# A decoder block on one core: high weight parts by a casting transfer of GpSimd's queue

## The chip, the cores and the metric

The kernel runs on one core of a Trainium2 chip, in one launch. The metric is device time in microseconds, the median of the runs. A profile of one execution stands beside it: engines are TensorE (PE, with its weight loads as PEld), VectorE (DVE), ScalarE (ACT), GpSimd (POOL) and SyncE (SP). SP and POOL issue transfers: SP on a hardware queue (q1 in the profile), POOL on a software queue (q0).

## The reference

One layer over 512 positions of width 1024, everything in float32:

```
h = rmsnorm(x)
[q | k | v | u_pool | u_gate] = h @ w_in            # 1024 x (1024+1024+1024+512+2048)
A = diff_attention(q, k, v)                         # 8 heads, two softmaxes each, causal
P = multiscale_pool(u_pool)                         # 4 groups, windows 2, 4, 8, 16
x = x + (sigmoid(g_A) * A + sigmoid(g_P) * P) @ w_out
x = x + relu(rmsnorm(x) @ w_up)^2 @ w_down          # 1024 -> 4096 -> 1024
return rmsnorm(x)
```

## The kernel before

Every product is made from parts: a float32 operand is split into a high part in the format float32r, which PE multiplies in one pass, and a low part, the rest, in the same format. A product is then three matmuls, high by high, high by low and low by high. Weights come in blocks of 128 x 1024 (512 KB), and each block has a high tile `wh_...` and a low tile `wl_...`. Both have four buffers that are used in turn, so a block's tiles can be filled while the three blocks before it are multiplied.

There are two ways to split a block, both in `get_w`. `load_w` issues a raw copy on SP's queue into a raw tile (`wr_...`, two buffers of tag `wr`; every third load, by the counter `nraw`, takes the one buffer of tag `wr3` while the first stage's memory is open) and allocates the high and low tiles.

- With an engine given (V for DVE), `split_w` casts the raw tile to the high one on ACT (L112) and subtracts on DVE (L113). This is the way of the query and key blocks (`proj` called by `qk`), of the four blocks of the second half of the output columns and of blocks 1 and 3 of the first half.
- With "dma" given, ACT casts the raw tile to the high one (L120), ACT writes its negative into the low tile (L121), and POOL issues a transfer that adds the weights from HBM once more onto the low tile (L122). This is the way of the 4 blocks of the pool branch (`pool`, tiles `wh_u`), the 16 gate blocks (`gate`, tiles `wh_ga` and `wh_gp`) and blocks 0 and 2 of the first half of the output columns (tiles `wh_o`): 22 blocks.

A projection block (`proj`, `mm3`) runs 16 matmuls of 512 columns with the high tile (L131, L132) and then 8 with the low one (L135). An output block (`mm_rows`, L581 to L583) takes high, low, high in turn, so it needs both tiles at once.

The stages in order of time: the norm and the value projection (to about 58 us); queries, keys, pool branch, gates and attention, head by head, with the pool and gate blocks as fillers between the heads by the list `LAG` (to 300 us); the output product in two halves of columns and the second norm (to about 350 us); then the up and down projections in four rounds, with their sums and differences of blocks also made by transfers of POOL's queue. Per head, POOL also computes two elementwise products for the norm of the head's output (L426, L427), whose result PE reads at L430, the window sums of the pool branch (L452) and a gate product (L481).

The order of instructions on each engine is not written by hand. A planner at build time simulates the engines, starts instructions as they become ready and allocates buffers; a few `after` edges fix an order where the text wants one. At run time each engine works strictly in that order and waits on semaphores, POOL's transfers included.

Of the kernel before, what the change touches and what calls it, by code (L numbers as in the profile page):

```python
# [12 lines left out]
F32R = mybir.dt.float32r  # L13
# [5 lines left out]
P = 128  # L19
# [32 lines left out]
def block_kernel(ctx, tc, xT, x_tok, gains, pos, consts, w_in, w_v, w_pool, w_out, w_up, w_dn, out):  # L52
    nc = tc.nc
    V, A, G, T = nc.vector, nc.scalar, nc.gpsimd, nc.tensor
# [12 lines left out]
    wp = ctx.enter_context(tc.tile_pool(name="wp", bufs=1))  # L67
# [22 lines left out]
    def f(ap):  # L90
        return ap.bitcast(F32)
# [4 lines left out]
    def load_w(src, name, nsplit=1, parts=None):  # L96

        nraw[0] += 1
        third = nraw[0] % 3 == 0 and ctx1_open
        raw = (tp if third else wp).tile([P, 1024], F32, tag="wr3" if third else "wr", name=f"wr_{name}", bufs=1 if third else 2)  # L100
        if nsplit == 1:
            nc.sync.dma_start(out=raw, in_=src)
        else:
            w = 1024 // nsplit
            for i in range(nsplit)[parts or slice(None)]:
                nc.sync.dma_start(out=raw[:, i * w : (i + 1) * w], in_=src[:, i * w : (i + 1) * w])
        hi = wp.tile([P, 1024], F32R, tag="wh", name=f"wh_{name}", bufs=4)
        lo = wp.tile([P, 1024], F32R, tag="wl", name=f"wl_{name}", bufs=4)
        return raw, hi, lo

    def split_w(raw, hi, lo, sl=slice(0, 1024), eng=None):
        ins = A.copy(out=hi[:, sl], in_=raw[:, sl])  # L112
        (eng or G).tensor_tensor(out=lo[:, sl], in0=raw[:, sl], in1=f(hi)[:, sl], op=ALU.subtract)  # L113
        return ins

    def get_w(src, name, eng=None):
        raw, hi, lo = load_w(src, name)
        if eng == "dma":

            A.copy(out=hi, in_=raw)  # L120
            A.mul(out=lo, in_=f(hi), mul=-1.0)  # L121
            G.dma_start(out=lo, in_=src, accum_op=ALU.add)  # L122
        else:
            split_w(raw, hi, lo, eng=eng)
        return hi, lo

# [15 lines left out]
    for i in range(2):  # L142
# [22 lines left out]
        out=mask[:, 384:512], in_=mask[:, 384:512], pattern=[[-1, P]],  # L165
# [51 lines left out]
    for n in range(2):  # L217
        accs = [bank((0, 1, 2, 3, 4, 5, 6, 0)[4 * n + t], f"v{n}_{t}") for t in range(NT)]
        for kk in range(4):
            if n == 0:  # L220
                xprep(2 * kk)
            if n == 0 and kk == 0:
                raw, hi, lo = wv0
                nc.sync.dma_start(out=raw[:, 512:], in_=w_v[0, 0, :, 512:])
            else:
                raw, hi, lo = load_w(w_v[n, kk], f"v{n}_{kk}", 2 if n == 0 else 1)
# [33 lines left out]
        for t in range(NT):  # L260
# [4 lines left out]
                out=vd[2], in0=av, scalar=rcol[:, t, 0:1], in1=vd[1],  # L265
# [26 lines left out]
        out=r_, in0=posf.rearrange("p (t o) -> p t o", o=1).to_broadcast(sh),  # L292
# [63 lines left out]
    def proj(m, name, eng=None):  # L356
        hi, lo = get_w(w_in[m], name, eng)
        a_ = acc(name)
        mm3(a_, hi, lo, xh, xl)
        return a_  # L360
# [245 lines left out]
    for kk in range(4):  # L606
        w = get_w(w_out[0, kk], f"o0_{kk}", V if kk % 2 else "dma")
        for k in (2 * kk, 2 * kk + 1):
            for t in range(NT):
                mm_rows(po[t], t, k, w, k == 0, k == NK - 1)  # L610
    for t in range(NT):
        nc.sync.dma_start(out=x1[:, t, :], in_=x_tok[t])
    for t in range(NT):
        x1_add(t, 0, po[t])
        row_early(t, 0)
    g2b, _ = gain(R[4].rearrange("p b c -> p (b c)"), 0)
    ws = [get_w(w_out[1, kk], f"o1_{kk}", V) for kk in range(4)]
    for t in range(NT):
        a_ = bank(4 + t, f"po1_{t}")
# [19 lines left out]
        for b in range(t // 2, 2):  # L639
            hi, lo = (gab[b][:, t // 2, i, :, sl] for i in range(2))  # L640
# [352 lines left out]
```

## Time and profile before

| | |
|---|---|
| median of 3 runs | 676.17 us (675.97 to 676.85) |
| span of the profiled execution | 675.2 us |
| PE busy | 665.3 us, 99% |
| DVE, ACT, POOL busy | 529.1, 462.5, 123.0 us |
| moved by q0 (POOL) and q1 (SP) | 38.80 MB and 69.38 MB |

The profiled execution has only its span of 675.2 us, from the first instruction to the last; the median is about 1 us above it. In the views below, a window row gives the stretch, its length, the busy time of PE, PEld, DVE, ACT and POOL with counts, then the granted PE clock, the busy share of the DMA engines and GB/s. A row of waits gives who waited for whom: us in total, times, longest. A group row gives line, engine, operation, tiles (written <- read), count, then busy us and mean ns of one. A row of one tile or line gives durations as minimum/median/maximum in ns. Rows in order of time begin with start and duration in us.

### The profile page before, as it was taken

How to read it: one execution, taken by the hardware profiler on the slowest of the kernel's cores; microseconds unless marked ns; L12 is line 12 of the kernel's file. 1: busy time of each engine (PE TensorE's matmuls, PEld its weight loads, DVE VectorE, ACT ScalarE, POOL GpSimd, SP SyncE). 2: the span in 40 equal slices, each digit the busy share in tenths (PEclk: the TensorE clock that was granted, in tenths of full speed). 3: DMA queues.
4: the chain of work that ended last, by engine and by line, in shares of the span. 5: the costliest groups of instructions: out<-in, count | busy, mean ns of one | idle time of the engine just before them, and what ended most of it. 6: DMA issues, size and time to landing. Idle time of an engine off the chain costs nothing.

```text
span 675.2 us, 9995 instructions
## 1 busy us (share of the span) xinstructions
PE 665.3 (99%) x3686; PEld 579.9 (86%) x3686; DVE 529.1 (78%) x879; ACT 462.5 (68%) x741; POOL 123.0 (18%) x137
## 2 busy tenths in 40 slices
PE   9999999999999999999999999999999999999995
PEld 7788888888888888888889988899889998899884
DVE  6955877799979986975478989667994599747995
ACT  8465587978887698883477975367753696356874
POOL 6201110132133212520201020202103021210120
PEclk9999999999999999999999999999999999999999
DMA  8526574435254364574964678676969579493863
GB/s 272 189 71 182 126 152 125 102 94 126 87 139 105 101 171 94 126 193 177 309 194 79 196 172 241 153 179 155 234 190 197 200 156 260 125 213 131 213 125 124
DMA packets 32880, 109.34 MB, mean 162 GB/s; under 512 B 4032, under 2 KB 4928, under 8 KB 32832
## 3 DMA queue, kind: packets, MB, share of 16 engines
q0 software_dynamic: 10656, 38.80, 32.4%
q1 hardware_dynamic: 21744, 69.38, 29.0%
q8 instruction: 29, 0.48, 0.3%
q10 hardware_dynamic: 432, 0.52, 0.2%
q14 instruction: 19, 0.16, 0.1%
HBM read 106.59 MB, written 2.10 MB: 161 GB/s over the span
## 4 chain that ended last, share of the span: by engine, by line
PE 86%; DMA 5%; issue 5%; DVE 1%; ACT 1%; SPq 0%; DVEq 0%; POOLq 0%
PE dm L838 7%; PE dm L840 7%; PE dm L841 7%; PE um L759 7%; PE um L764 7%; PE um L761 7%; DMA wga_uNone<-w_up 5%; PE o L417 2%; PE ga L132 2%; PE ga L131 2%; PE gp L135 2%; PE k L132 2%; PE gp L132 2%; PE gp L131 2%; PE k L131 2%
## 5 line engine op out<-in xcount | busy, mean ns | idle before, releaser
L840 PE MATMUL dm<-wh_dt,z 128*128 128x512 f32 (+1 forms) x128 | 49.5, 387 | 0.0
L841 PE MATMUL dm<-wl_dt,z 128*128 128x512 f32 (+1 forms) x128 | 49.4, 386 | 0.0
L838 PE MATMUL dm<-wh_dt,z 128*128 128x512 f32 (+1 forms) x128 | 49.0, 387 | 0.0
L759 PE MATMUL um<-gss,wh_ut 128*128 128x256 f32 x192 | 48.1, 284 | 0.1
L761 PE MATMUL um<-gss,wh_ut 128*128 128x256 f32 x192 | 48.1, 283 | 0.0
L400 ACT ACTIVATE p<-p,st 128x128 f32<-128x128 f32 (+3 forms) x64 | 35.8, 560 | 14.1 <-DVE st L396 13.8
L112 ACT CAST wh_ut<-wga_uNone 128x1024 fp32r<-128x1024 f32 x24 | 24.9, 1053 | 28.8 <-PE dm L840 19.2
L856 DVE TENSOR_TENSOR x<-x,dm 128x512 f32<-128x512 f32 x48 | 32.8, 687 | 14.1 <-PE dm L841 14.0
L670 POOL DMA_DIRECT2D wga_dNone<-w_dn x16 | 14.2, 887 | 151.8 <-DVE wl_dt L113 151.8
L113 DVE TENSOR_TENSOR wl_ut<-wga_uNone,wh_ut 128x1024 fp32r<-128x1024 f32 x24 | 29.0, 1224 | 12.5 <-ACT wh_ut L112 12.5
L112 ACT CAST wh_ub<-wr_u 128x1024 fp32r<-128x1024 f32 x24 | 25.1, 1051 | 19.0 <-PE um L761 10.1
L670 POOL DMA_DIRECT2D wga_uNone<-w_up x18 | 15.6, 867 | 120.9 <-DVE wl_ut L113 86.9
L840 PE MATMUL dm<-wh_db,z 128*128 128x512 f32 x96 | 37.2, 389 | 0.0
L841 PE MATMUL dm<-wl_db,z 128*128 128x512 f32 x96 | 37.2, 389 | 0.0
L759 PEld LDWEIGHTS um<-gss,wh_ut 128*128 128x128 f32 x192 | 36.8, 192 | 0.3 <-ACT rawz L776 0.3
L761 PEld LDWEIGHTS um<-gss,wh_ut 128*128 128x128 f32 x192 | 36.9, 192 | 0.0
L838 PE MATMUL dm<-wh_db,z 128*128 128x512 f32 x96 | 35.8, 390 | 0.0
L113 DVE TENSOR_TENSOR wl_ub<-wr_u,wh_ub 128x1024 fp32r<-128x1024 f32 x24 | 29.2, 1222 | 7.9 <-ACT wh_ub L112 7.9
L112 ACT CAST wh_dt<-wga_dNone 128x1024 fp32r<-128x1024 f32 x24 | 24.8, 1050 | 14.6 <-issue 4.1
L735 DVE TENSOR_TENSOR z<-rawz,z 128x1024 fp32r<-128x1024 f32 x28 | 33.7, 1225 | 0.9 <-ACT z L732 0.9
L396 DVE CUSTOM_DVE_ANT_0 p<-s,mask 128x128 f32<-128x128 f32 (+3 forms) x64 | 30.3, 485 | 3.4 <-PE s L395 3.3
L732 ACT CAST z<-rawz 128x1024 fp32r<-128x1024 f32 x28 | 28.7, 1048 | 6.0 <-DVE rawz L741 4.9
(324 smaller groups left out, 2222.9 us busy)
## 6 DMA issues: line engine op xcount, KB each, us to landing
wr_u<-w_up SPq DMA_DIRECT2D x24, 512.0 KB, 5.3
wr_d<-w_dn SPq DMA_DIRECT2D x24, 512.0 KB, 4.2
wga_uNone<-w_up POOLq DMA_DIRECT2D x18, 512.0 KB, 6.7
wga_dNone<-w_dn POOLq DMA_DIRECT2D x16, 512.0 KB, 5.8
wr_k<-w_in SPq DMA_DIRECT2D x8, 512.0 KB, 3.3
wr_ga<-w_in SPq DMA_DIRECT2D x8, 512.0 KB, 3.3
wr_gp<-w_in SPq DMA_DIRECT2D x8, 512.0 KB, 4.2
wl_ga<-w_in POOLq DMA_DIRECT2D x8, 512.0 KB, 5.5
```

The source lines that it names most:

```text
L112: ins = A.copy(out=hi[:, sl], in_=raw[:, sl])
L113: (eng or G).tensor_tensor(out=lo[:, sl], in0=raw[:, sl], in1=f(hi)[:, sl], op=ALU.subtract)
L131: T.matmul(acc, lhsT=hi[:, c], rhs=rh[:, k, :], start=k == 0, stop=False)
L132: T.matmul(acc, lhsT=hi[:, c], rhs=rl[k], start=False, stop=False)
L400: A.activation(out=pr[:, c, :N], in_=pr[:, c, :N], func=AF.Exp, scale=-1.0, bias=st[:, c : c + 1], accum_out=st[:, 2 + c : 3 + c])
L735: V.tensor_tensor(out=z[:, 1], in0=r, in1=f(z[:, 0]), op=ALU.subtract)
L759: m = T.matmul(a_, lhsT=hi[:, c], rhs=rh[:, k, :], start=p + k == 0 and onto is None, stop=False, skip_group_check=True)
L761: T.matmul(a_, lhsT=hi[:, c], rhs=rl[:, k, :], start=False, stop=False, skip_group_check=True)
L764: m = T.matmul(a_, lhsT=lo[:, c], rhs=rh[:, k, :], start=False, stop=k == 3, skip_group_check=True)
L838: m = T.matmul(a_, lhsT=zh, rhs=hi[:, sl], start=p == 0 and start, stop=False, skip_group_check=True)
L840: T.matmul(a_, lhsT=zl, rhs=hi[:, sl], start=False, stop=False, skip_group_check=True)
L841: end = T.matmul(a_, lhsT=zh, rhs=lo[:, sl], start=False, stop=p == 3, skip_group_check=True)
```

## The change

In `get_w`, the "dma" way no longer calls `load_w`. It allocates the high and low tiles itself, lets a transfer of POOL's queue bring the weights from HBM into the high tile, where the change of type from float32 to float32r makes it a casting transfer, and goes on as before: ACT writes the negative, POOL's second transfer adds the weights. The raw tile, its copy on SP's queue, the count in `nraw` and ACT's cast fall away for the 22 blocks. The other way is the same.

```diff
     def get_w(src, name, eng=None):
-        raw, hi, lo = load_w(src, name)
         if eng == "dma":
-
-            A.copy(out=hi, in_=raw)
+            hi = wp.tile([P, 1024], F32R, tag="wh", name=f"wh_{name}", bufs=4)
+            lo = wp.tile([P, 1024], F32R, tag="wl", name=f"wl_{name}", bufs=4)
+            G.dma_start(out=hi, in_=src)
             A.mul(out=lo, in_=f(hi), mul=-1.0)
             G.dma_start(out=lo, in_=src, accum_op=ALU.add)
         else:
+            raw, hi, lo = load_w(src, name)
             split_w(raw, hi, lo, eng=eng)
         return hi, lo
```

## The prediction

> **What bounds the kernel now.** I read the page's busy line first, then the windows by stage, then who TensorE (PE) waits for.
>
> ```profile
> PE 665.3 (99%) x3686; PEld 579.9 (86%) x3686; DVE 529.1 (78%) x879; ACT 462.5 (68%) x741; POOL 123.0 (18%) x137
> ```
> ```profile
> 0.00:25.00 25.00, 23.37 (x98) 19.38 (x99) 19.31 (x23) 18.21 (x33) 15.37 (x24) 1.00 0.73 243
> ...
> 75.00:300.00 225.00, 224.94 (x1089) 187.97 (x1088) 190.53 (x441) 183.32 (x347) 59.07 (x58) 1.00 0.50 121
> 300.00:350.00 50.00, 50.00 (x233) 41.56 (x232) 29.33 (x48) 25.89 (x47) 4.76 (x5) 1.00 0.74 237
> 350.00:400.00 50.00, 49.01 (x378) 46.92 (x379) 44.18 (x51) 41.05 (x62) 6.97 (x8) 1.00 0.59 146
> ...
> 650.00:675.20 25.20, 18.00 (x91) 15.22 (x89) 17.11 (x41) 12.47 (x35) 0.00 (x0) 0.94 0.40 120
> ```
> ```profile
> PE warm L170 <- POOL onesr L159: 1.1, 1, 1.1
> PE h2T L629 <- ACT h2f L646: 0.6, 1, 0.6
> PE um L759 <- ACT gss L602: 0.3, 1, 0.3
> PE v L237 <- DVE con L282: 0.3, 1, 0.3
> PE v L235 <- ACT wh_v L112: 0.2, 1, 0.2
> ```
>
> The columns of the windows are PE, weight loads, DVE, ACT, POOL, granted clock, DMA share and GB/s. The changed transfers feed blocks that PE multiplies in the stretch 75 to 315 us. There PE is busy 224.94 us of 225 and 50.00 of 50, at clock 1.00. The waits of PE name no weight of the pool branch, of a gate or of the first output columns: 2.5 us in all, none of it in a touched place. What PE loses lies at the two ends (1.6 us in the first 25 us, 7.2 us in the last 25) and one microsecond between 350 and 400, and the diff is in none of the three. So the kernel is a PE stream without holes where it is changed: a saving on ACT, SP or the queues is not time unless it shortens the stream, and an operand that comes late is time at once.
>
> A busy PE is not PE at its peak, so I bound what a hidden wait could still be worth by the mean duration of one multiplication of 512 columns, in the touched stage (gate and key blocks) and in the down projection:
>
> ```profile
> L131 PE MATMUL ga<-xh,wh_ga 128*128 128x512 f32 x64 | 25.3, 395 | 0.0
> L131 PE MATMUL k<-xh,wh_k 128*128 128x512 f32 x64 | 25.1, 392 | 0.0
> ...
> L840 PE MATMUL dm<-wh_dt,z 128*128 128x512 f32 x124 | 48.3, 390 | 0.0
> ```
>
> Gate against down projection, that is 5 ns for one; over the 1089 matmuls of 75 to 300 us it is 5.4 us. It is the most that a better fed PE could win there, and most of it is not waiting: the long ones follow on short transposes and scores of attention, which stay.
>
> **The change part by part.** 22 blocks take the "dma" way: 4 of the pool branch, 16 gates, 2 of the first output columns.
>
> ```profile
> L120 ACT CAST wh_gp<-wr_gp x8: 1036/1046/1055, 78.6 to 275.0; 128x1024 fp32r<-128x1024 f32 x8
> ...
> L121 ACT ACTIVATE wl_gp<-wh_gp x8: 1054/1062/1067, 80.1 to 278.3; 128x1024 fp32r<-128x1024 f32 x8
> ...
> L122 POOL DMA_DIRECT2D wl_gp<-w_in x8: 847/876/889, 82.6 to 279.6; - x8
> ...
> DMA to landing us min/median/max: 5.2/5.4/7.2
> ```
> ```profile
> 60.00:300.00 240.00, 21.95 (x21) 1.00 0.51 124
> ```
> ```profile
> q0 software_dynamic: 3117, 11.39, 28.7%
> q1 hardware_dynamic: 5184, 18.09, 22.3%
> ...
> wr_gp<-w_in SPq DMA_DIRECT2D x8, 512.0 KB, 4.2
> ```
>
> *Cast removed.* 22 casts of ACT by 1.046 us are 23.0 us; the second row, L120's own time from 60 to 300 us, has 21.95 for 21 of them. ACT is busy 183.32 of 225 us, so this lowers it to about 162. On the path that sets the end it is worth 0: PE never waited for such a cast. What ACT and DVE then do sooner (softmax, weight splits) PE takes no sooner, because it is full.
>
> *Raw copy removed.* 22 issues leave SP's queue, and the raw buffers (two of one tag, every third load in another) turn among the q, k and remaining output blocks alone, which come earlier. The count that picks every third load runs over fewer calls, so other loads get the third buffer. Worth 0: nothing on PE waited for a raw copy.
>
> *Casting transfer added.* 22 issues on POOL by 0.876 us are 19.3 us, and POOL is busy 59.07 of 225. How long one takes to land the trace does not show by itself. From below it is the raw copy of the same 512 KB by SP's queue, 4.2 us median (gp); from above the accumulating transfer of POOL's queue, 7.2 us at the most; the median 5.4 I take, because that one has the same queue, the same source and the same float32 to float32r pair, and only reads its destination besides. On the DMA engines the two queue rows of 60 to 300 us give the price: 28.7% of 240 us for 11.39 MB is 3.2 us of all sixteen for one block of 0.524 MB, 22.3% for 18.09 MB is 1.55. The move costs between 0 and 22 x 1.65 = 36 us of engine time, so the DMA share of that stretch goes from 0.51 to 0.66 at the most: room enough, 0 on the path.
>
> *New chain before PE.* Before, a block's cast started as soon as its high buffer was free. Afterwards that moment starts a transfer: issue and landing 5.4, negation on ACT 1.06, accumulating transfer 5.4 = 11.9 us until the low part is there, with the 0.88 us of an issue and a wait of about 1 us behind ACT's work some 13.8 us. The cover is the four buffers in turn. How long it is, two late blocks show (ACT's order of time, then PE's):
>
> ```profile
> 274.98 1.05 ACT L120 CAST wh_gp<-wr_gp 128x1024 fp32r<-128x1024 f32 x1
> ...
> 279.61 1.05 ACT L120 CAST wh_o<-wr_o 128x1024 fp32r<-128x1024 f32 x1
> ```
> ```profile
> 288.42 0.39 PE L131 MATMUL ga<-xh,wh_ga 128*128 128x512 f32 x1
> ...
> 294.48 0.40 PE L131 MATMUL gp<-xh,wh_gp 128*128 128x512 f32 x1
> ...
> 295.31 0.48 PE L430 MATMUL ss<-sql,onesr 128*128 128x512 f32 x1
> ...
> 298.83 1.98 PE L135 MATMUL gp<-xh,wl_gp 128*128 128x512 f32 x8
> 300.65 0.39 PE L581 MATMUL po<-wh_o,vh 128*128 128x512 f32 x1
> 300.87 0.39 PE L582 MATMUL po<-wl_o,vh 128*128 128x512 f32 x1
> ```
>
> The gate's cast starts at 274.98 and PE reads its high part at 294.48, its low part at 298.83: cover 19.5 and 23.9 us. The output block's starts at 279.61, and PE reads the low part at 300.87, right behind the high one: cover 21.3. Less the chain, 10.1 and 7.5 us stay for queueing on POOL. If that cover were gone, each microsecond of lateness would be a microsecond of the span.
>
> *What stands behind the new waits on POOL.* POOL works in order. It now also waits for a high buffer (released by PE), and its wait for the negation includes a landing. Queued behind are the window sums of the pool branch (L452), the gate products (L481), and the two that PE wants soon, L426 and L427, the squares of a head's output:
>
> ```profile
> 275.29 1.48 POOL L452 TENSOR_TENSOR pa<-u 128x512 f32<-128x512 f32 x1 [2.46 <-DVE u L444]
> 276.84 1.10 POOL L452 TENSOR_TENSOR pb<-pa 128x512 f32<-128x512 f32 x1
> 278.03 1.04 POOL L452 TENSOR_TENSOR pa<-pb 128x512 f32<-128x512 f32 x1
> 279.61 0.87 POOL L122 DMA_DIRECT2D wl_gp<-w_in  x1 [0.54 <-ACT wl_gp L121]
> 280.22 1.58 POOL L452 TENSOR_TENSOR pb<-pa 128x512 f32<-128x512 f32 x1
> 283.77 1.67 POOL L481 TENSOR_TENSOR o<-o,g 128x512 f32<-128x512 f32 x1 [1.96 <-DVE o L435]
> 285.38 0.88 POOL L122 DMA_DIRECT2D wl_o<-w_out  x1
> 291.58 1.12 POOL L426 TENSOR_TENSOR sqo<-o 128x512 f32<-128x512 f32 x1 [5.32 <-ACT o L421]
> 292.78 2.16 POOL L427 TENSOR_TENSOR sql<-sqo,sqh 128x512 fp32r<-128x512 f32 x1
> 296.08 0.88 POOL L122 DMA_DIRECT2D wl_o<-w_out  x1 [1.15 <-ACT wl_o L121]
> ```
>
> L427 ends at 294.94 and PE reads its result at 295.31 (the ss row above): 0.4 us to spare. But POOL had idled 5.32 us in front of L426. The order of every engine is laid out at build time by a planner that starts what is ready, so as a rule a high transfer goes out while POOL would idle, ahead of an accumulation that is not due. I take 0 here.
>
> The sum: 0 from ACT, 0 from SP, 0 from the DMA engines, 0 from POOL's order. The profiled span is 675.2 us and the median of the runs 676.17, about 1 us more around it. Forecast 676.2 us. A difference of 0.2%, 1.35 us, is about what can be told from none here: "same" is 674.8 to 677.5.
>
> **The rivals.**
>
> *Slower: POOL's order.* A pair whose accumulation waits for its own landing stands in front of L426 when the head's output is ready, or the pairs run one at a time. The first place: the hold is at most 5.4 + 1.06 = 6.5 us, less the 0.4 spare of the late head up to 6.1 us on PE; half of that, 3 us, if the output is ready midway. The second: pairs strictly one at a time take 5.4 + 1.06 + 0.88 = 7.3 us, while PE takes a block each 6.1 us there (288.42, 294.48, 300.65), so the last six such blocks in a row lose 6 x 1.2 = 7 us, about the 7.5 to spare; the ten POOL rows above bring 10.2 us of other work (L452, L481, L426, L427), and from the moment that some 2 us of it cannot be hidden, PE waits. Price again 1.5 to 6 us. Likeliest 679.2, up to 683. Against it: POOL's 18% share, and waits that today pass without a hole in PE.
>
> The Trainium skill, "SBUF — State Buffer", section "SBUF: two separate sides", says that descriptors of a POOL transfer cannot be written while DVE holds the port they share, and gives an example in which a transfer grows from about 0.62 to 3.1 us. By it, an estimate, each of the two transfers of a chain would come 2.5 us later, the 7.5 us to spare would fall to 2.5, and I would give this rival 4 chances in 10. The trace bears it out only weakly: with DVE busy 190.53 of 225 us, the landings stay between 5.2 and 7.2 and the issues between 847 and 889 ns.
>
> *Faster: ACT was the feeder after all.* If the 23 us off ACT remove the small stretches in the matmuls, at most 5.4 us go; a quarter is the threshold. Price 673.5 with a third of it gone. For it: nothing but the 395 against 390 ns. Against it: no wait on PE, and the key blocks, which take no transfer of POOL's, have 392 ns and so most of the same stretch.
>
> *The transfer is not as cheap as its neighbour.* If a casting copy took twice the 5.4 us, the chain would be 19 us and the output block's spare 2 us. PE would still be fed in most blocks; 677 to 679.
>
> **How the numbers follow.** Same 0.60 (676.2; own range 674.8 to 677.5). Slower 0.30: POOL's order 0.25, the dear transfer 0.05. Faster 0.10. The range: about half of the faster cases stay above 674.2, and two thirds of the slower below 681, so 674.2 to 681.0 leaves out some 15 in 100.
>
> **What would show it.** Right: PE busy 99% with 665 us, no wait on a wh or wl of ga, gp, u or o; ACT at about 440 us, 22 casts fewer; POOL with 22 more issues, landing at 4 to 6 us; q1 down and q0 up by 11.5 MB. Wrong: PE waiting for sql (L430), or for wh_o or wl_o near 300 us, with POOL's L122 and the new line waiting longest in front of it; or PE matmuls of the stage at 390 ns and a shorter span.

## The result, and the profile after

The changed kernel takes 688.66 us (687.63 to 690.22, four runs) against 676.48 us for the kernel before: ratio 1.0179 [1.0165, 1.0193]. It is slower by 12 us, beyond the range of the prediction (674.2 to 681.0). In the changed kernel L120 is the high transfer, L121 the negation, L122 the accumulating transfer; most later lines have one more than before.

The page's span, busy line and queue rows (queue: packets, MB, share of the span of the 16 DMA engines), then the queue rows of the kernel before:

```profile
span 686.3 us, 9956 instructions
...
PE 669.3 (98%) x3686; PEld 581.8 (85%) x3686; DVE 529.5 (77%) x879; ACT 439.5 (64%) x719; POOL 135.3 (20%) x159
...
q0 software_dynamic: 13824, 50.34, 37.0%
q1 hardware_dynamic: 18576, 57.84, 23.7%
```
```profile
q0 software_dynamic: 10656, 38.80, 32.4%
q1 hardware_dynamic: 21744, 69.38, 29.0%
```

The span grew by 686.3 - 675.2 = 11.1 us. PE is busy 4.0 us longer with the same 3686 matmuls, and idle for 17.0 instead of 9.9 us, 7.1 us more; 4.0 + 7.1 is the growth. The windows say where (columns as before):

```profile
75.00:300.00 225.00, 217.62 (x1033) 179.87 (x1032) 181.78 (x427) 155.23 (x315) 68.09 (x75) 0.98 0.46 112
...
250.00:275.00 25.00, 19.96 (x91) 15.57 (x89) 16.17 (x46) 15.11 (x34) 6.62 (x8) 0.93 0.55 124
```

In the touched stage PE did 1033 matmuls where it had done 1089, and 25 us of it, 250 to 275, stand out: 91 matmuls, 5.0 us idle, clock 0.93. Those 25 us had 121 matmuls before:

```profile
250.00:275.00 25.00, 24.94 (x121) 20.82 (x121) 17.41 (x48) 21.97 (x40) 6.24 (x6) 1.00 0.58 121
```

The rows of who PE waits for name no weight there, but the softmax:

```profile
PE t L410 <- DVE p L406: 4.7, 4, 3.0
PE u L132 <- DVE g L474: 1.2, 1, 1.2
...
PE po L583 <- DMA wl_o<-w_out: 0.8, 1, 0.8
```

The 3.0 us hole is followed back engine by engine, in rows in order of time: PE, then DVE, then ACT, then POOL.

```profile
256.29 0.45 PE L410 MATMUL t<-ident,p 128*128 128x128 f32 x1 [3.02 <-DVE p L406]
```
```profile
250.54 0.28 DVE L397 CUSTOM_DVE_ANT_0 p<-s,mask 128x128 f32<-128x128 f32 x1
...
255.80 0.35 DVE L406 SCALAR_TENSOR_TENSOR p<-p,st 128x128 f32<-128x128 f32 x1 [0.53 <-ACT p L405]
```
```profile
252.47 1.06 ACT L121 ACTIVATE wl_u<-wh_u 128x1024 fp32r<-128x1024 f32 x1 [3.19 <-DMA wh_u<-w_in]
253.44 0.39 ACT L401 ACTIVATE p<-p,st 128x128 f32<-128x128 f32 x1
...
255.36 0.40 ACT L405 ACTIVATE p<-p,st 128x128 f32<-128x128 f32 x1 [1.07 <-DVE st L404]
```
```profile
245.17 0.86 POOL L122 DMA_DIRECT2D wl_gp<-w_in  x1 [7.49 <-ACT wl_gp L121]
245.72 0.87 POOL L120 DMA_DIRECT2D wh_u<-w_in  x1
253.82 0.85 POOL L122 DMA_DIRECT2D wl_u<-w_in  x1 [7.23 <-ACT wl_u L121]
254.37 0.87 POOL L120 DMA_DIRECT2D wh_ga<-w_in  x1
261.87 0.85 POOL L122 DMA_DIRECT2D wl_ga<-w_in  x1 [6.64 <-ACT wl_ga L121]
```

PE is dry because L406 is late, L406 because ACT's softmax (L401, L405) is late, and the softmax begins the moment the negation in front of it, L121, is through. The scores that the softmax reads had been ready since 250.8 us (DVE's L397), while ACT stood idle. L121 had stood 3.19 us waiting for `wh_u` to land. That transfer had gone out late, at 245.72, because on POOL it stands right behind the accumulation of the block before, which had waited 7.49 us for ACT. It is a ring: ACT waits for POOL's transfer, and POOL's next transfer waits for ACT. A turn of it, from accumulation to accumulation, takes 253.82 - 245.17 = 8.65 and then 261.87 - 253.82 = 8.05 us.

A turn does not always cost PE something. The ring also turned at 83 to 100 us (accumulations at 83.03, 91.15 and 99.79), and 17.3 of the 27.0 us that ACT waited for landings lie before 100 us; PE, from 60 to 110 us, was idle for 0.3 us. What covered the softmax there and not at 253 us was not tried.

The hole costs more than its length. After it, the same PE rows go on at another pitch:

```profile
256.97 0.63 PE L133 MATMUL k<-xlb,wh_k 128*128 128x512 f32 x1
257.39 0.63 PE L132 MATMUL k<-xh,wh_k 128*128 128x512 f32 x1
...
259.36 0.39 PE L133 MATMUL k<-xlb,wh_k 128*128 128x512 f32 x1
259.59 0.34 PE L395 MATMUL s<-ks,qs 128*128 128x384 f32 x1
```
```profile
255.00:260.00 5.00, 3.71 (x12) 3.07 (x13) 3.73 (x12) 1.47 (x4) 0.23 (x1) 0.66 0.95 210
```

Starts are 0.43 us apart (256.97 to 257.39) until about 259.1, then 0.23 us again (259.36 to 259.59); the granted clock of these 5 us is 0.66. The Trainium skill, "TensorE: Matmul & The Clock Gate", section "Part 1: The HAM clock gate (the "warmup" mystery)", says that PE falls to half its clock after an idle window of about 3.4 us and that matmuls of 512 columns then start 426.7 instead of 215.7 ns apart. The trace has the lower clock and 0.43 against 0.23 us, but after a hole of 3.02 us, shorter than that window. A second group of small gaps (270 to 276 us: softmax, a key cast and the gate input `g`, all of ACT and DVE) is followed by the same 0.43 us pitch up to 279.6.

### The profile page after: what moved, and what is told of

Its sections match the earlier page's. It is cut to its first block, busy times and chain, and to the rows that moved or that the text cites. A ratio compares the mean times of both kernels' runs of the same rounds, so it can differ in the third digit from the quotient of the medians.

```text
span 686.3 us, 9956 instructions
## 1 busy us (share of the span) xinstructions
PE 669.3 (98%) x3686; PEld 581.8 (85%) x3686; DVE 529.5 (77%) x879; ACT 439.5 (64%) x719; POOL 135.3 (20%) x159
## 3 DMA queue, kind: packets, MB, share of 16 engines
q1 hardware_dynamic: 18576, 57.84, 23.7%
## 4 chain that ended last, share of the span: by engine, by line
PE 58%; DVE 11%; DMA 11%; issue 11%; ACT 6%; POOL 2%; SPq 0%; POOLq 0%; ACTq 0%; DVEq 0%
PE dm L839 7%; PE dm L841 7%; PE dm L842 7%; PE um L765 6%; PE um L760 6%; PE um L762 6%; DMA wga_uNone<-w_up 5%; PE v L236 2%; PE v L238 2%; PE v L237 2%; DMA wh_gp<-w_in 2%; DMA wh_ga<-w_in 2%; DVE p L406 1%; ACT p L401 1%; DVE p L397 1%
## 5 line engine op out<-in xcount | busy, mean ns | idle before, releaser
L401 ACT ACTIVATE p<-p,st 128x128 f32<-128x128 f32 (+3 forms) x64 | 35.6, 557 | 20.7 <-DVE st L397 20.3
L671 POOL DMA_DIRECT2D wga_dNone<-w_dn x16 | 14.2, 885 | 153.4 <-DVE wl_dt L113 153.4
L857 DVE TENSOR_TENSOR x<-x,dm 128x512 f32<-128x512 f32 x48 | 32.4, 679 | 14.6 <-PE dm L842 14.6
L113 DVE TENSOR_TENSOR wl_ut<-wga_uNone,wh_ut 128x1024 fp32r<-128x1024 f32 x24 | 29.1, 1222 | 11.1 <-ACT wh_ut L112 11.1
L113 DVE TENSOR_TENSOR wl_dt<-wga_dNone,wh_dt 128x1024 fp32r<-128x1024 f32 x24 | 29.1, 1217 | 4.3 <-ACT wh_dt L112 4.3
L762 PE MATMUL um<-gab,wh_ub 128*128 128x256 f32 x128 | 32.3, 283 | 0.0
```

What stands on the lines that cost most here:

```text
L401: A.activation(out=pr[:, c, :N], in_=pr[:, c, :N], func=AF.Exp, scale=-1.0, bias=st[:, c : c + 1], accum_out=st[:, 2 + c : 3 + c])
L671: return [G.dma_start(out=tiles[c], in_=src[q, b, c], accum_op=ALU.add) for c in range(2)]
L762: T.matmul(a_, lhsT=hi[:, c], rhs=rl[:, k, :], start=False, stop=False, skip_group_check=True)
L857: V.tensor_tensor(out=xs, in0=xs, in1=pa[a], op=(ALU.add, ALU.subtract)[n])
```

## The experiments

Theory A: ACT works in order, the negation now waits for a landing, and what PE needs from ACT stands behind it. Against it stand B, that the cost is POOL's, whose transfers go one pair at a time, so that the weights come late, and C, that it is simply the load of 22 more transfers on POOL's queue. A ratio is against the kernel before on the same chip, with its 95% interval in brackets. Every edit makes the planner lay all engines out anew, so I take 1 to 3 us between kernels for no evidence of a cause. The diffs show the lines that matter: `...` stands for code left out, and so are the lines that set up spare tiles, the list of the blocks and the helper `high`.

### The negation taken away from ACT, and its operand made early

**neg_on_pool**: POOL writes the negative itself.

```diff
-            A.mul(out=lo, in_=f(hi), mul=-1.0)
+            G.tensor_scalar(out=lo, in0=f(hi), scalar1=-1.0, scalar2=None, op0=ALU.mult)
```

> The negation of the high part goes from ACT to POOL; all else as after the change. Theory A (ACT, which works in order, stands at the negation until the high transfer has landed, and the softmax behind it comes late to PE): ACT no longer waits for a landing (27 us of such waits in the changed kernel go to 0), the softmax is on time, 677 to 681 us. Theory B (the pairs run one at a time on POOL, and the weights themselves come late): each pair gets longer by the POOL instruction, some 2 us, so it gets worse, 690 us or more, with PE waiting for wl or wh. Theory C (the casting transfers load POOL or the DMA engines): nothing changes, 686 to 690.

Measured 680.32 us, 1.0047 [1.0032, 1.0062]. ACT waits for no high transfer of a pool, gate or output block. POOL now waits for the landings and takes about 3 us for a negative (2.8 to 3.3); PE's longest wait in the stage is a head's squares behind that, 1.5 us. The forecast that B has for this kernel, 690 us or more, failed: POOL's high transfers still go one after another (245.13, 252.00 and 259.23 us), and PE's waits name no weight of the new way.

**neg_of_constant**: ACT's instruction stays, with a constant tile as its operand instead of the high tile, so the low part is not the reference's. All transfers stay.

```diff
-            A.mul(out=lo, in_=f(hi), mul=-1.0)
+            A.mul(out=lo.rearrange(...), in_=ident.rearrange(...).to_broadcast([P, 8, P]), mul=-1.0)
```

> ACT negates a constant tile into the low tile, so neither ACT nor the accumulating transfer waits for the landing; all 44 transfers stay, and so does ACT's instruction. (The low parts of the 22 blocks hold the weight less a constant.) Theories A and B: the loss is gone, 676 to 678 us. Theory C (load of the transfers): stays at 686 to 690.

Measured 679.88 us, 1.0041 [1.0028, 1.0054]. With every transfer in place but no wait of ACT for one, 8.8 of the 12.2 us are gone (688.66 against 679.88). So the load of the transfers and ACT's instruction count are at most a few us together. But both edits also open the ring: no transfer of POOL's waits for ACT to have met a landing. So they do not tell a wait on ACT from a wait that sits in a ring.

### The ring opened, with the negation on ACT

**high_first_on_pool** issues the next block's high transfer ahead of this block's accumulation. **high_first_neg_later** has the same order of transfers on POOL; only the edge that makes the planner do so hangs on the negation instead of on the accumulation, which also puts the negation later among ACT's work.

```diff
+            nsrc, nname = next_dma.get(name, (None, None))
+            if nname:
+                hq.append(high(nsrc, nname))      # G.dma_start of the next high tile
             A.mul(out=lo, in_=f(hi), mul=-1.0)
-            G.dma_start(out=lo, in_=src, accum_op=ALU.add)
+            add = G.dma_start(out=lo, in_=src, accum_op=ALU.add)
+            if nname:
+                after(add, hq[0][1])              # high_first_neg_later: after(neg, hq[0][1])
```

> The high transfer of the next block is issued on POOL ahead of the accumulation of this one, by program order and an edge; the negation stays where the planner puts it. Theory B (POOL's order): 676 to 678. Theory A (ACT's wait): the high transfer goes out earlier, but ACT's negation may still stand in front of its landing; between 677 and 684, and the remaining loss goes with ACT's waits for wh. Theory C: 686 to 690.

> As the kernel with the next high transfer ahead, but the edge is on the negation: it comes on ACT after the next high transfer has been issued in the plan, about a block later. Theory A: no wait of ACT for a landing, 676 to 678, at or below the one with the early negation. Theory B: the same as that one. Theory C: 686 to 690.

Measured 684.59 us, 1.0111 [1.0096, 1.0127], and 677.35 us, 1.0009 [0.9999, 1.0018]. ACT's waits for landings from 60 to 310 us, of the first kernel and then of the second:

```profile
ACT wl_ga L138 <- DMA wh_ga<-w_in: 8.7, 4, 2.6
ACT wl_gp L138 <- DMA wh_gp<-w_in: 6.0, 2, 3.5
ACT wl_u L138 <- DMA wh_u<-w_in: 3.7, 2, 3.4
ACT wl_o L138 <- DMA wh_o<-w_out: 0.3, 1, 0.3
```
```profile
ACT wl_u L138 <- DMA wh_u<-w_in: 3.5, 1, 3.5
ACT wl_ga L138 <- DMA wh_ga<-w_in: 2.2, 1, 2.2
```

Both pass the high transfers in the same order; 18.7 us of waiting on ACT against 5.7, and 7.2 us of time. By these sums it looks like A, but the trace of the first kernel does not bear it out. Its longest hole of PE, in the rows of PE, DVE, POOL and ACT, then all of L402:

```profile
224.60 0.30 PE L414 MATMUL s<-ks,qs 128*128 128x128 f32 x1 [2.40 <-DVE ks L402]
```
```profile
221.23 3.95 DVE L402 TENSOR_TENSOR ks<-q1k,kz 64x512 fp32r<-64x512 f32 x2
```
```profile
221.28 1.63 POOL L501 TENSOR_TENSOR o<-o,g 128x512 f32<-128x512 f32 x1
222.52 1.38 POOL L472 TENSOR_TENSOR pa<-pb 128x512 f32<-128x512 f32 x1
```
```profile
224.41 1.06 ACT L138 ACTIVATE wl_ga<-wh_ga 128x1024 fp32r<-128x1024 f32 x1 [2.57 <-DMA wh_ga<-w_in]
```
```profile
L402 DVE TENSOR_TENSOR ks<-q1k,kz x16: 674/690/3225, 75.3 to 269.5; 64x512 fp32r<-64x512 f32 x16
```

PE waited for a DVE instruction that took 3.2 us where its median is 0.69, while POOL did two of its products; ACT had finished its own part of the key before it began to wait for the landing. The next longest hole, 1.6 us before 180.97, also follows L402 (3.2 us for two). These two are 4.0 of the 4.4 us that PE idled from 75 to 300 us. So the 7.2 us are not shown to be the price of ACT's waits. The second kernel is the best form of the change that I found; it equals the kernel before and does not beat it.

**act_reads_too** puts the negation on POOL and lets ACT read the high tile as well, into a spare tile.

```diff
-            A.mul(out=lo, in_=f(hi), mul=-1.0)
+            A.mul(out=state["scr"], in_=f(hi)[:, 0:768].rearrange(...), mul=-1.0)
+            G.tensor_scalar(out=lo, in0=f(hi), scalar1=-1.0, scalar2=None, op0=ALU.mult)
```

> As the kernel with the negation on POOL (680.3), and ACT also reads the high part of each of the 22 blocks into a spare tile that nothing reads (768 columns, some 0.8 us each). The weights do not depend on it; only ACT's wait for the landing comes back, with 18 us of work on an ACT that has room. Theory A: the loss is back, 685 to 692, with ACT waiting for landings and PE for the softmax. Theory B (lateness of the weights): stays at 680 to 682.

Measured 686.65 us, 1.014 [1.0124, 1.0155]. The size looks like A, the place does not:

```profile
75.00:300.00 225.00, 223.71 (x1082) 186.75 (x1081) 191.21 (x436) 156.32 (x322) 121.27 (x97) 1.00 0.51 119
```

ACT waited for landings here too (8.0 us for `wh_gp`, 5.7 for `wh_u`), yet PE had only 1.3 us of idle in the stage; the loss lies at the output product (2.8 us for `wl_o`) and behind it (3.3 us of idle from 350 to 400). In this kernel no accumulation of POOL's waits for ACT, and one high transfer is put down to it (6.0 us). So waits on ACT without the ring were covered, and the run is no support for A alone.

**free_accumulation** and **free_accumulation_in_place** open the ring on the other side: the accumulation goes into a spare tile, so that it needs nothing of ACT (the low part then is only the negative, ready at once, and the transfer has 384 KB instead of 512, so more than the ring is changed). The second ties it behind the negation in the planner's order.

```diff
-            A.mul(out=lo, in_=f(hi), mul=-1.0)
-            G.dma_start(out=lo, in_=src, accum_op=ALU.add)
+            neg = A.mul(out=lo, in_=f(hi), mul=-1.0)
+            after(G.dma_start(out=state["scr"], in_=src[:, 0:768].rearrange(...), accum_op=ALU.add), neg)
```

> After the change, but the accumulating transfer goes to a spare tile (384 KB) and waits neither for ACT nor for the landing; ACT's negation of the high part remains and is the whole low part (the low parts of the 22 blocks miss the weight). So POOL is free and the high transfer goes out when its buffer is free; ACT still waits for a landing where the plan has it too early. Theory B: 676 to 678. Theory A: as far as ACT's waits for landings stay; 677 to 683, and the rest goes with these waits.

> After the change, but the accumulating transfer (384 KB) goes to a spare tile behind the negation in the plan and waits neither for it nor for the landing (the first try had them all at the start); the low parts of the 22 blocks are the negated high parts alone. POOL issues the next high transfer as soon as its buffer is free. Theory B: 676 to 678. Theory A: the landings come earlier, ACT waits for less than the 27 us, and the time is above 677 in proportion to what is left of it.

The first, without the tie, says little: the planner put all accumulations at the start, the first high transfer went out at 81.71 us, and it took 718.19 us, 1.0604 [1.0583, 1.0625]. The second took 677.44 us, 1.0009 [0.9994, 1.0024], B's number and not A's, although ACT waited 24.3 us for landings, nearly as long as in the changed kernel (10.5 + 9.9 + 6.6 = 27.0). First its waits of ACT, then those of the changed kernel, then the order of time of POOL in this kernel:

```profile
ACT wl_u L121 <- DMA wh_u<-w_in: 8.1, 3, 3.6
ACT wl_gp L121 <- DMA wh_gp<-w_in: 6.9, 4, 4.4
ACT wl_ga L121 <- DMA wh_ga<-w_in: 5.5, 4, 1.8
ACT wl_o L121 <- DMA wh_o<-w_out: 3.8, 2, 2.2
```
```profile
ACT wl_gp L121 <- DMA wh_gp<-w_in: 10.5, 3, 5.4
ACT wl_ga L121 <- DMA wh_ga<-w_in: 9.9, 4, 2.9
ACT wl_u L121 <- DMA wh_u<-w_in: 6.6, 2, 3.4
```
```profile
244.31 0.59 POOL L120 DMA_DIRECT2D wh_u<-w_in  x1 [5.06 <-PE ga L133]
...
250.53 0.58 POOL L120 DMA_DIRECT2D wh_ga<-w_in  x1 [4.40 <-PE q L133]
...
257.05 0.58 POOL L120 DMA_DIRECT2D wh_gp<-w_in  x1 [4.41 <-PE k L133]
```

The high transfers here wait for PE to release a buffer and follow each other every 6.2 and 6.5 us; in the changed kernel they follow ACT, every 8.65 and 8.05. So A as I had put it, that ACT's wait is a price by itself, falls, as B had with neg_on_pool. My reading is that the wait costs when the next landing depends on ACT in its turn, so that lateness is handed on from block to block instead of being made up.

### The same wait put into the kernel before

Both twins leave the kernel before as it is and add 22 casting transfers of 384 KB into a spare tile and 22 small copies on ACT. In **twin_no_wait** the copy reads the old high tile; in **twin_act_waits** it reads the tile that the transfer fills, which also makes the next transfer wait for ACT: the ring.

```diff
+            after(G.dma_start(out=state["scr"], in_=src[:, 0:768].rearrange(...)), cast)
+            A.copy(out=state["out"], in_=f(hi)[:, 0:256].rearrange(...))     # twin_no_wait
+            A.copy(out=state["out"], in_=f(state["scr"])[:, :, 0:128])       # twin_act_waits
```

> The kernel before, its weights made as before; for each of the 22 blocks POOL also casts 384 KB into a spare tile, placed beside the block's cast (the first try had all of these at the start), and ACT copies 256 columns of the high part, which it has just made itself, into another spare place. This is the load of the change without a wait of ACT for a landing. Theory A: 676 to 679. Theory C (load of POOL and DMA engines): 683 or more.

> The twin: the same transfers and the same small copy on ACT, but the copy reads the spare tile that the transfer fills, so ACT waits for a landing in its order where the planner places it. No weight depends on it. Theory A: ACT's waits for landings are back, and the time is 3 to 10 us above the twin's. Theory B (lateness of the weights) and C: no difference between the twins beyond 1 us.

Measured 679.14 us, 1.0038 [1.0026, 1.005], and 693.35 us, 1.0242 [1.0208, 1.0275]. The stage's window of the first, then of the second, and ACT's wait in the second:

```profile
75.00:300.00 225.00, 223.21 (x1077) 185.80 (x1076) 188.84 (x438) 185.86 (x365) 71.74 (x77) 1.00 0.62 152
```
```profile
75.00:300.00 225.00, 213.44 (x998) 173.70 (x997) 178.57 (x412) 174.86 (x343) 67.03 (x72) 0.98 0.56 139
```
```profile
ACT wt L124 <- DMA wt<-w_in: 22.6, 10, 5.4
```

The transfers themselves cost at most the 2.4 us of the first. What the copy reads, and nothing else in the kernel's text, makes 14.2 us, more than I had expected; PE again waits for the softmax (`PE t L416 <- DVE p L412`, 4.6 us). So an edit that puts ACT's wait and the ring in is enough for a loss of this size; it does not split the two. The trace does not put all of it behind ACT either: two of the holes, 1.0 us before 156.32 and 1.9 us before 226.27, follow DVE instructions that took 2.06 and 1.86 us where others of their kind took 0.67 and 0.75.

**extra_transfers** was to price the load: the kernel before with 22 such transfers and no copy.

```diff
+            G.dma_start(out=state["scr"], in_=src[:, 0:768].rearrange(...))
```

> The kernel before, with one more transfer of POOL's queue for each of the 22 blocks (384 KB, cast to float32r, into a spare tile that nothing reads): POOL's issues and the traffic without the dependence. Theory C (load): 684 or more. Theories A and B: 676 to 679.

Measured 691.37 us, 1.0206 [1.0172, 1.024], and it says nothing on the load: with no tie the planner put all 22 one behind the other from 6 to 107 us, most of them far ahead of their blocks, and PE had one hole of 12.6 us near 100 us (a score behind DVE). twin_no_wait answers the question.

### Part of the blocks

**six_blocks** gives the new way to the pool and output blocks alone; **but_last_group** to the first 15 blocks, with the last pool block, its four gates and the output blocks as before.

```diff
-        if eng == "dma":
+        if eng == "dma" and name[0] == "g":     # but_last_group: u3, ga6, gp6, ga7, gp7 and o blocks
+            raw, hi, lo = load_w(src, name)
+            ...
+        elif eng == "dma":
```

> Only the pool branch and the output blocks (6 of 22) take the casting transfer, the 16 gates the old way. Theory A: the six stand alone, each with at most one wait of ACT of some 3 us, mostly covered: 676 to 680. Theory B: no pairs in a row, 676 to 678. Theory C: 6/22 of the loss, about 680.

> The casting transfer for the first 15 blocks alone; the last group of the pool branch with its four gates, and the two output blocks, go the old way. The large hole of PE in the changed kernel (250 to 285 us) is where this group is made. Theory A, with the pile-up in the last run of blocks: 677 to 679, about 10 of the 12 us gone. If the loss were spread evenly over the blocks, 15/22 of it would stay: 685.

Measured 679.05 us, 1.0033 [1.0019, 1.0048], and 694.44 us, 1.0263 [1.0246, 1.028]. The first lies in A's range (676 to 680) and within some 1 us of what B and C had, so it tells none from another. The second came out against its forecast. The hole at 250 to 300 did go (1.3 us of idle are left there), but another opened at the output product (windows of this kernel, then PE's longest wait):

```profile
310.00:315.00 5.00, 0.00 (x0) 0.00 (x0) 0.69 (x1) 0.97 (x2) 0.43 (x1) 0.84 1.05 308
315.00:320.00 5.00, 4.81 (x11) 3.80 (x12) 0.56 (x1) 0.00 (x0) 0.00 (x0) 0.50 0.73 297
```
```profile
PE po L588 <- DMA wl_o<-w_out: 6.2, 1, 6.2
```

The second accumulation of `wl_o` was issued at 305.22, 9.1 us later than in the kernel before (296.08), because it stood 11.2 us behind ACT's negation; the slower of the two landings took 9.9 us. The output blocks are built here as in the kernel before, where the landings took 5.2 to 5.3 us. I read it as the planner's new order at the seam of two stages; that was not tried by a run.

### What is shown and what stays open

Shown: the 22 transfers and ACT's instructions as such cost little (neg_of_constant, twin_no_wait); taking ACT's wait for the landings away, and the ring with it, brings back 8.3 and 8.8 of the 12.2 us (neg_on_pool, neg_of_constant); putting both into the kernel before makes 14.2 us; and in the changed kernel the longest hole of PE goes back, row by row, to such a wait on ACT. With the ring open and ACT still waiting, free_accumulation_in_place is 0.1% above the kernel before (24.3 us of waits), and act_reads_too has 1.3 us of PE's idle in the stage.

Argued, but not shown: that it is the ring which makes the waits dear. The early turns of it cost PE next to nothing, and free_accumulation_in_place changes more than the ring. Open: the 3 to 4 us that neg_on_pool and neg_of_constant leave; how much of ACT's wait a given schedule covers; why DVE instructions such as L402 run long at times, which is where PE's idle in high_first_on_pool comes from; and the losses of act_reads_too and but_last_group at the output product, for which only their profiles suggest a reason.

## Why the prediction was wrong, step by step

- *What bounds the kernel.* Right: PE has no slack from 75 to 315 us. Its sentence on a late operand, one microsecond of span for each of lateness, was too low: 7.1 us more of idle came with 4.0 us more of busy time, some 3.0 of it in the two stretches at 0.43 us a start.
- *Cast and raw copy removed, worth 0.* Right: ACT is down from 462.5 to 439.5 us (22 instructions fewer), q1 down from 69.38 to 57.84 MB, and no gain shows from either.
- *Casting transfer: landing 5.4 us, engine time 0 to 36 us.* Right, but for single landings: they took 3.5 to 6.7 us, the shortest below the bound of 4.2. Landings by their medians, from 60 to 300 us:

```profile
wh_ga<-w_in POOLq DMA_DIRECT2D x8, 512.0 KB, 5.9
wl_ga<-w_in POOLq DMA_DIRECT2D x8, 512.0 KB, 5.4
wh_gp<-w_in POOLq DMA_DIRECT2D x8, 512.0 KB, 4.3
```

  Over the whole span (queue rows under the result) q0's time rose from 32.4% of 675.2 to 37.0% of 686.3 us, by 35.2 us for 22 blocks: 1.60 us of all sixteen engines for a block. q1's fell by 33.2 us, 1.51 for a raw copy. So a casting transfer costs about what the raw copy did and not the accumulation's 3.2, and the move costs 2 us of engine time, near the lower end of 0. The accumulations still land in 5.3 to 5.5 us by their medians, beside a DVE busy 181.78 of 225 us, so the 2.5 us more for each transfer did not come that the prediction had worked out by the Trainium skill, "SBUF — State Buffer", section "SBUF: two separate sides".
- *New chain before PE: 13.8 us, with "a wait of about 1 us behind ACT's work".* The length held: `wh_u` was issued at 245.72 and its accumulation at 253.82; with the median landing of 5.4 us that is 13.5 us, and PE read the low part only at 283.5. **The wait in it failed, with the next step.** Its direction was wrong: ACT waits for the transfer, by 27.0 us over 9 negations, and in the turns shown the accumulation on POOL then waits 6.6 to 7.5 us for ACT.
- *What stands behind the new waits on POOL.* **This is the step that failed.** It asked the question for POOL alone. The negation on ACT got a new wait as well, and behind it stands the softmax that PE reads next; the prediction never names what is queued there. Its reason for taking 0, that "a high transfer goes out while POOL would idle, ahead of an accumulation that is not due", is the opposite of the order found where PE lost its time: from 245 to 293 us each of the six high transfers stands right behind an accumulation that waits for ACT. What it cost: 3.0 us of PE's idle before 256.29 and, by the two runs without ACT's wait, 8.3 and 8.8 of the 12.2 us.
- *The rival "POOL's order".* The nearest to what came: strictly serial pairs, at 7.3 us each, price up to 683. The turns took 8.65 and 8.05 us: from the issue to the end of ACT's wait 6.75 and 6.15 (the rival has 5.4), from there through the negation to the accumulation's issue 1.35, to the next high transfer 0.55. What PE missed was not the weights but the softmax. Of its named signs, PE did not wait for `sql`, and for `wl_o` it waited 0.8 us. Against it the prediction set "waits that today pass without a hole"; in the kernel before, ACT's rows from 60 to 310 us name no landing, so those waits told nothing of a wait on ACT.

## What to carry to other kernels

For every wait that a change adds, list what is queued behind it on *that* engine, on each engine that gets one, and look for rings: if engine 1 waits for a transfer of queue 2 and the next transfer of queue 2 waits for engine 1, a late block makes the next one late, and averages of load say nothing. By my reading, moving work to an idle queue only pays when the consumer of the landing sits on an engine whose next instructions nobody needs soon, or late enough in that engine's order; here 24.3 us of waiting on ACT cost nothing that shows once POOL's next transfer no longer hung on ACT. Before a gain is credited to an edit, follow PE's holes back in the trace: in high_first_on_pool the sum of ACT's waits fitted the theory, and the holes had another cause. When a load is priced by adding transfers, tie them in place, or a planner will gather them where they mean something else.

## What was not expected of the hardware

A hole of 3.0 us in a busy PE is followed by about 2.7 us at starts of 0.43 instead of 0.23 us. A casting transfer of 512 KB costs the DMA engines about what a plain copy does (1.60 against 1.51 us of all sixteen) and half of an accumulating one (3.2). A DVE instruction of 64 partitions by 512, 0.69 us by its median, took 3.2 us while POOL did two products of 128 by 512; why was not tried. An accumulating transfer of an output block, 5.2 to 5.3 us in the kernel before, took up to 9.9 us in but_last_group, in a stretch that moved some 280 to 310 GB/s; traffic alone does not explain it, since the kernel before moved 277 and 351 GB/s in the two windows (295 to 305 us) in which its second one landed.
